# Queries and keys turned block by block, and maxima over partitions without GpSimd

## The chip, the cores and the metric

One core of a Trainium2 chip runs the kernel. The metric is the device time of one launch in microseconds (us), from the first to the last instruction of the core and what lies around them. Lower is better.

## The reference

Two layers of a hybrid backbone for 2048 latent tokens and 256 context tokens (2304 together, context first) with 1024 channels. Cut to what matters here:

```python
def hybrid_layer(h, hc, ...):                       # called twice
    lat = split_cols((rms_norm(h, norm_g) * (1 + scale) + shift) @ w_in)     # 1024 -> 3584
    cx  = split_cols((rms_norm(hc, norm_g) * (1 + scale_c) + shift_c) @ w_in)
    att_l, att_c = gqa_branch(lat[4], lat[5], lat[6], cx[4], cx[5], cx[6], q_g, k_g, cos, sin, need_ctx)
    hg_l, hg_c = hgrn_branch(...)                   # gated recurrence in both directions
    y_conv, y_four, g_att, g_hg = mix_stream(lat, conv_w)   # short convolution, 2-D Fourier, gates
    y = concatenate([y_conv, att_l * g_att, hg_l * g_hg, y_four]) @ w_out
    return h + gate * y, ...

def gqa_branch(...):                                # 4 query heads, 2 key heads, 64 wide
    ql = apply_rope(rms_norm(to_heads(q_l, 4), q_g), cos, sin)
    kl = apply_rope(rms_norm(to_heads(k_l, 2), k_g), cos, sin)
    # latent queries attend to latent and context keys; context queries to context keys
    # (the context output is needed in the first layer only)
```

Everything is float32 in the reference. The kernel does its large products in float16 pairs (a high part and what is left over), with power-of-two scales that are taken from the largest absolute value of a tensor.

## The kernel before

One instruction stream per engine is written out by nested generators (`weave` interleaves several by their shares of the work), and a list scheduler may then move instructions of independent tiles past each other. DMAs all go through SyncE's queue (SPq in the profile).

A layer goes through these stages: a recurrence stage over nine blocks of 256 tokens (`hg_proj`, `hg_levels`, with the norms of the next tokens), the reverse recurrence (`hg_reverse`), the Fourier branch, a stage that makes the attention's queries, keys and values and the gates (`att_block`, `gate_block`), and then attention in jobs of 512 queries, woven with the convolution blocks and the output projection. The first layer's attention stage runs from about 700 us to 1370 us, the second's from about 2040 us to the end.

**Weights.** Each of the 14 blocks of `w_in` per layer goes through `wprep`: two loads of 512 KB into `wst` (line 368), `wsplit` takes the largest absolute value of each partition on VectorE (line 142, two instructions, joined in line 378), `allmax` takes the maximum over the 128 partitions with a GpSimd all-reduce (line 136), `pow2` makes the scale (lines 124 to 130), and ScalarE and VectorE write the high and low part (lines 389, 390). `allmax` is called 32 times in all: for 28 weight blocks, for the two layers' modulation (`mod_finish`) and for the two layers' values (`att_load`).

**GpSimd's other work.** `rpow` (line 151) takes the power -0.5 on GpSimd, for the norms (`nrr`), for the recurrence's output (`hrr`, used in line 739) and for queries and keys (`arr`, used in line 828).

**Queries and keys.** After `att_rope` a block's keys are stored token by token into the DRAM tensor `d_k` with the columns (high, high, low) and padding, the queries into `d_qt` likewise (lines 852, 859, 860: two, two and two stores per block). The padding itself, zeros and two columns of 64, is written by 36 small stores at the start (`load_masks`, lines 231 and 232). When attention opens, `att_load` turns the keys with four transposing DMAs from DRAM (line 869) and `att_fetch` turns the queries of a job with one (line 888: 512 tokens by 1024 columns). `att_max` (line 901) finds each query's largest score; its results go by DMA into two more rows of the second query operand (lines 920, 923), so that the second score product (line 977) subtracts them.

Of the kernel before, what the change touches and what calls it, by code (L numbers as in the profile page):

```python
# [4 lines left out]

# [7 lines left out]
F16 = mybir.dt.float16  # L13
F32 = mybir.dt.float32
# [4 lines left out]
ALU = mybir.AluOpType  # L19
# [6 lines left out]
NCX = 256  # L26
# [47 lines left out]
class Net:  # L74
# [57 lines left out]
        return s[:, 0:1], s[:, 1:2]  # L132

    def allmax(self, a):
        r = self.t(self.small, [128, 1], F32, "allmax")
        self.nc.gpsimd.partition_all_reduce(r, a, channels=128, reduce_op=bass_isa.ReduceOp.max)
        return r

    def absmax(self, src, pool=None):
# [15 lines left out]
    def setup(self):  # L155
# [4 lines left out]
        nc.vector.tensor_copy(out=self.id16, in_=self.id32)  # L160
        self.mhalf = cst.tile([128, 24], F32, name="mhalf")
        nc.vector.memset(self.mhalf, -0.5)
        self.pshift = cst.tile([128, 1], F32, name="pshift")
        nc.vector.memset(self.pshift, PSHIFT)
        self.cact = cst.tile([128, 32, 8], F32, name="cact")
# [48 lines left out]
        self.d_op = dt("d_op", [NT, 256])  # L214
        self.d_qb = dt("d_qb", [NTT, 128, 256])

        self.d_qt = dt("d_qt", [NT, 2, 4, 128], F16)
        self.d_k = dt("d_k", [NT, 2, 256], F16)
        self.d_v = dt("d_v", [NTT, 128, 128])
        self.d_gate = dt("d_gate", [2, 2, D])  # L220

    def load_masks(self, pool):
        nc = self.nc
        nc.sync.dma_start(out=self.masks, in_=self.ap["masks"])

        pad = self.t(pool, [128, 2, 4, 64], F16, "pad", 1)
        nc.gpsimd.memset(pad, 0.0)
        nc.gpsimd.memset(pad[:, 1, 0:2, 0:2], MROW)
        for t in range(NTT):
            r = slice(t * 128, t * 128 + 128)  # L230
            nc.sync.dma_start(out=self.d_qt[r, 1, :, 64:128], in_=pad[:, 0])
            nc.sync.dma_start(out=self.d_k[r, :, 192:256], in_=pad[:, 1, 0:2])


    def mod_load(self, l, c0, n, pool, bufs=2):
# [136 lines left out]
    def wsplit(self, l, b, half, pool=None, pace=False):  # L372

        nc = self.nc
        slow = self.paced if pace else ExitStack
        with slow():
            am = self.absmax(half[0])
            nc.vector.tensor_tensor(out=am, in0=am, in1=self.absmax(half[1]), op=ALU.max)
            ds = self.t(self.small, [128, 4], F32, "ds", bufs=16)
            sw, isw = self.pow2(self.allmax(am), self.small, tag="sw")  # L380
            nc.vector.tensor_copy(out=ds[:, 3:4], in_=isw)
        yield
        for i, st in enumerate(half):
            with slow():
                if i == 0:
                    wh = self.t(pool or self.wpool, [128, KC, 256], F16, "wh")
                    wl = self.t(pool or self.wpool, [128, KC, 256], F16, "wl")
                k = slice(4 * i, 4 * i + 4)
                a = nc.scalar.activation(out=wh[:, k], in_=st, func=AF.Copy, scale=sw)  # L389
                v = nc.vector.scalar_tensor_tensor(out=wl[:, k], in0=st, scalar=sw, in1=wh[:, k], op0=ALU.mult, op1=ALU.subtract)  # L390
            if i == 0:
                yield
        self.W[b] = (wh, wl, ds)
        self.wlast = (a, v)
        if self.mod[l] is not None:
            self.wscale(l, self.W[b])
        yield
# [367 lines left out]
    def att_open(self, l, pool):  # L765
        nc = self.nc
        self.atp = pool
        self.apend = []
# [12 lines left out]
        nc.vector.scalar_tensor_tensor(out=self.ascale, in0=inv[0], scalar=0.125, in1=inv[1], op0=ALU.mult, op1=ALU.mult)  # L781
        self.rope = self.t(pool, [128, 2, 16, 32], F32, "rope", 1)
        nc.sync.dma_start(out=self.rope, in_=self.ap["rope"])

    def att_block(self, l, sb):
# [15 lines left out]
        if needq:  # L801
            h0 = 0
            pq = self.bank("mm")
            for j in range(2):
                yield from self.mm_tok(pq[:, j * 256 : j * 256 + 256], wq, sb * 2 + j)
            nc.scalar.activation(
                out=x[:, :, 0:4], in_=pq.rearrange("p (j h d) -> p j h d", j=2, h=4), func=AF.Copy, scale=wq[2][:, 0:1]
            )
        nh = 6 - h0
        xv = x[:, :, h0:6]  # L810
        sq = self.t(pool, [128, 2, 6, 64], F32, "asq", 2)
# [10 lines left out]
    def att_rope(self, sb, x, r, h0):  # L822
# [20 lines left out]
                nc.vector.tensor_tensor(out=tmp, in0=xp[:, :, :, :, 1], in1=tab(1 - e), op=ALU.mult)  # L843
                nc.vector.tensor_tensor(out=yp[:, :, :, :, e], in0=yp[:, :, :, :, e], in1=tmp, op=o)

        kt = self.t(pool, [128, 2, 2, 192], F16, "akt", 2)
        yk = y[:, :, 4:6]
        nc.vector.tensor_copy(out=kt[:, :, :, 0:64], in_=yk)
        nc.vector.tensor_copy(out=kt[:, :, :, 64:128], in_=kt[:, :, :, 0:64])
        nc.vector.tensor_sub(out=kt[:, :, :, 128:192], in0=yk, in1=kt[:, :, :, 0:64])  # L850
        for j in range(2):
            nc.sync.dma_start(out=self.d_k[sb * 256 + j * 128 : sb * 256 + j * 128 + 128, :, 0:192], in_=kt[:, j])
        if h0 == 0:
            q = self.t(pool, [128, 2, 4, 128], F16, "aqt", 2)
            nc.vector.tensor_copy(out=q[:, :, :, 64:128], in_=y[:, :, 0:4])
            nc.vector.tensor_sub(out=q[:, :, :, 0:64], in0=y[:, :, 0:4], in1=q[:, :, :, 64:128])
            for j in range(2):
                r = slice(sb * 256 + j * 128, sb * 256 + j * 128 + 128)
                nc.sync.dma_start(out=self.d_qt[r, 0], in_=q[:, j])
                nc.sync.dma_start(out=self.d_qt[r, 1, :, 0:64], in_=q[:, j, :, 64:128])  # L860

    def att_load(self, keep, pool):

        nc = self.nc

        self.K = self.t(keep, [128, 4, NT], F16, "K12", 1)
        self.V = self.t(keep, [128, NTT, 2, 129], F16, "V", 1)
        for a, b in ((0, NCX), (NCX, 768), (768, 1536), (1536, NT)):
            nc.sync.dma_start_transpose(out=self.K[:, :, a:b], in_=self.d_k[a:b].rearrange("t h x -> t (h x)"))
        nc.vector.memset(self.V[:, :, :, 64:65], 1.0)  # L870
        am = self.t(self.small, [128, 1], F32, "amax")
        nc.vector.tensor_reduce(out=am, in_=self.vmax, axis=AX.X, op=ALU.max)
# [9 lines left out]
    def att_fetch(self, job, pool):  # L882

        nc = self.nc
        n = job["nq"] * 128
        r = slice(job["tq"] * 128, job["tq"] * 128 + n)
        job["Q"] = self.t(pool, [128, 8, 512], F16, "Q12", 2)
        nc.sync.dma_start_transpose(out=job["Q"][:, :, :n], in_=self.d_qt[r].rearrange("t k h x -> t (k h x)"))
        yield

    def att_max(self, job, pool):

        nc = self.nc
        nq, nk, Q = job["nq"], job["nk"], job["Q"]
        chunks = [(c, min(512, nk * 128 - c)) for c in range(0, nk * 128, 512)]
        mx = self.t(pool, [128, 4, nq, len(chunks)], F32, "amx", 2)
        for j in range(nq):
            for h in range(4):
                for i, (c, w) in enumerate(chunks):
                    ps = self.bank("tr")  # L900
                    nc.tensor.matmul(ps[:, :w], lhsT=Q[:, h, j * 128 : j * 128 + 128], rhs=self.K[:, h // 2 * 2, c : c + w], start=True, stop=True)  # L901
# [15 lines left out]
        for e in range(2):  # L917
            src = mt[4 * nq * e : 4 * nq * e + 4 * nq]
            if nq == 4:
                nc.sync.dma_start(out=Q[64 + e : 65 + e, 4:8], in_=src)  # L920
            else:
                for h in range(4):
                    nc.sync.dma_start(out=Q[64 + e : 65 + e, 4 + h, : nq * 128], in_=src[nq * h : nq * h + nq])
        yield

    def att_core(self, job, pool):
# [1 line left out]
        nc = self.nc  # L928
        tq, nq, nk = job["tq"], job["nq"], job["nk"]
        n = nq * 128  # L930
        Q = job["Q"]
        dst = {}

        def values(h, s, ph, pl):
# [33 lines left out]
        for h in range(4):  # L968
            kv = h // 2
            for s in range(nk):  # L970
# [5 lines left out]
                nc.tensor.matmul(ps[:, :n], lhsT=self.K[:, 2 * kv, c], rhs=Q[:, h, :n], start=True, stop=False)  # L976
                nc.tensor.matmul(ps[:, :n], lhsT=self.K[:66, 2 * kv + 1, c], rhs=Q[:66, 4 + h, :n], start=False, stop=True)  # L977
# [335 lines left out]
    def layer(self, l, L, R, tail):  # L1313
# [33 lines left out]
        with ExitStack() as st:  # L1347
# [3 lines left out]
            if l == 0:  # L1351
# [11 lines left out]
                self.load_masks(nm)  # L1363
            else:
                self.wlast = ()
            self.hg_open(l, hgk)
# [18 lines left out]
        def late():  # L1385


            def gen():
                self.att_rope(*self.apend.pop(0))
                yield  # L1390

            return 1, gen()
# [180 lines left out]
```

## Time and profile before

| | |
|---|---|
| median of three runs | 2719.91 us (2716.54 to 2721.13) |
| the profiled execution, own time | 2729.11 us |
| its span, first to last instruction | 2727.3 us |
| mean granted TensorE clock | 0.979 of full speed |
| TensorE matmul busy | 2591.0 us (95%) |
| VectorE busy | 2060.0 us (76%) |
| ScalarE busy | 1495.7 us (55%) |
| GpSimd busy | 118.2 us (4%) |

Busy time of TensorE counts pipelined matmuls whose ends are modelled, so 95% says that it hardly ever has nothing in flight, not that it is at its peak. What to look for in this profile is the 136 us in which TensorE does nothing, and what it waits for then.

### The profile page before, as it was taken

The page shows a single profiled execution, that of the slowest core. Times are in us where ns is not written, and L with a number is a line of the kernel's source. Part 1 is how long each engine was busy: PE and PEld are TensorE (multiplying, and loading weights), DVE is VectorE, ACT ScalarE, POOL GpSimd, SP SyncE. Part 2 cuts the span into 40 slices and gives each one's busy share as a digit, 9 for nine tenths or more (in the row PEclk, how much of TensorE's full clock was granted, in tenths as well). Part 3 has the DMA queues.
Part 4 walks back from the last instruction along what each step waited for, and adds up shares of the span by engine and source line. Part 5 has one row for each costly group of instructions (what it writes and reads, how often), then busy time and mean ns, then how long its engine had stood idle before and what let it go on. Part 6 is the DMA issues. An engine that isn't in the chain of part 4 may idle for free.

```text
span 2727.3 us, 67225 instructions
## 1 busy us (share of the span) xinstructions
PE 2591.0 (95%) x28142; PEld 2045.1 (75%) x28142; DVE 2060.0 (76%) x4534; ACT 1495.7 (55%) x2823; POOL 118.2 (4%) x140
## 2 busy tenths in 40 slices
PE   5899999999899999999989999989998999999998
PEld 3788877788677876666678788878886787666677
DVE  5888864656686678898776888866678766999874
ACT  3777642322316557698736666523221655879872
POOL 0000001011000000000000000010110000000000
PEclk8899999999899999999999999999999999999999
DMA  8111168322610032312161111343324102221223
GB/s 238 62 49 52 33 199 269 119 81 77 145 35 25 24 102 81 99 57 75 65 210 63 45 49 36 105 136 120 85 76 88 44 24 59 95 77 57 75 83 109
DMA packets 260232, 240.32 MB, mean 88 GB/s; under 512 B 107093, under 2 KB 232025, under 8 KB 259929
## 3 DMA queue, kind: packets, MB, share of 16 engines
q1 hardware_dynamic: 259928, 236.04, 28.0%
q8 instruction: 220, 3.60, 0.6%
q14 instruction: 84, 0.68, 0.1%
HBM read 149.98 MB, written 72.30 MB: 82 GB/s over the span
## 4 chain that ended last, share of the span: by engine, by line
PE 67%; DVE 14%; ACT 6%; DMA 5%; issue 4%; SPq 2%; POOL 2%; POOLq 0%; DVEq 0%; ACTq 0%
PE psmm L1245 12%; PE psmm L414 6%; PE psmm L415 6%; PE psmm L416 6%; PE pstr L901 4%; PE psmm L430 4%; PE psmm L428 4%; PE psmm L429 4%; PE pspv L943 4%; PE pssc L976 4%; PE pssc L977 4%; PE pspv L944 2%; PE pspv L689 2%; ACT aP L979 1%; DMA wmod<-w_mod 1%
## 5 line engine op out<-in xcount | busy, mean ns | idle before, releaser
L414 PE MATMUL psmm<-xh,wh 128*128 128x256 f16 x2208 | 609.8, 276 | 13.8 <-DVE xh L344 7.0
L415 PE MATMUL psmm<-xl,wh 128*128 128x256 f16 x2208 | 608.6, 276 | 1.5 <-DVE xl L345 1.5
L416 PE MATMUL psmm<-xh,wl 128*128 128x256 f16 x2208 | 608.4, 276 | 0.0
L979 ACT ACTIVATE aP<-pssc,pshift,ascale 128x512 f32<-128x512 f32 (+1 forms) x584 | 446.4, 779 | 244.8 <-PE pssc L977 228.4
L986 DVE TENSOR_TENSOR apl<-aP,aph 128x512 f16<-128x512 f32 (+1 forms) x584 | 392.0, 682 | 104.6 <-ACT aph L985 97.1
L428 PE MATMUL psmm<-wh,xh 128*128 128x256 f16 x1664 | 456.0, 274 | 2.5 <-ACT wh L389 1.9
L902 DVE TENSOR_REDUCE amx<-pstr 128x1 f32<-128x512 f32 (+1 forms) x648 | 391.9, 627 | 87.0 <-PE pstr L901 84.5
L429 PE MATMUL psmm<-wl,xh 128*128 128x256 f16 x1664 | 455.4, 274 | 1.1 <-DVE wl L390 1.1
L430 PE MATMUL psmm<-wh,xl 128*128 128x256 f16 x1664 | 455.5, 274 | 0.0
L985 ACT CAST aph<-aP 128x512 f16<-128x512 f32 (+1 forms) x508 | 307.2, 620 | 10.3
L943 PE MATMUL pspv<-V,aph 128*128 128x129 f16 x2320 | 296.3, 222 | 0.4 <-ACT ao L954 0.4
L943 PEld LDWEIGHTS <-aph 128*128 128x128 f16 x2320 | 211.4, 97 | 83.0 <-issue 47.9
L944 PE MATMUL pspv<-V,apl 128*128 128x65 f16 x2320 | 269.6, 193 | 2.8 <-DVE apl L986 2.2
L415 PEld LDWEIGHTS <-wh 128*128 128x128 f16 x2208 | 218.3, 99 | 67.7 <-issue 14.5
L414 PEld LDWEIGHTS <-wh 128*128 128x128 f16 x2208 | 218.7, 99 | 56.2 <-issue 6.7
L901 PE MATMUL pstr<-K,Q 128*128 128x512 f16 (+1 forms) x648 | 229.3, 362 | 28.4 <-issue 19.7
L416 PEld LDWEIGHTS <-wl 128*128 128x128 f16 x2208 | 218.2, 99 | 34.8 <-issue 2.4
L944 PEld LDWEIGHTS <-apl 128*128 128x128 f16 x2320 | 208.4, 98 | 44.2 <-DVE apl L986 14.7
L1245 PE MATMUL psmm<-xh,oyh 128*128 128x512 f32 x544 | 239.2, 440 | 0.1
L1245 PE MATMUL psmm<-xl,oyh 128*128 128x512 f32 x544 | 238.5, 438 | 0.0
L976 PE MATMUL pssc<-Q,K 128*128 128x512 f16 (+1 forms) x584 | 221.8, 380 | 3.3 <-ACT aP L979 2.3
L977 PE MATMUL pssc<-Q,K 66*128 66x512 f16 (+1 forms) x584 | 222.6, 384 | 0.5 <-DMA Q<-amt 0.4
(279 smaller groups left out, 4304.4 us busy)
## 6 DMA issues: line engine op xcount, KB each, us to landing
wst<-w_in SPq DMA_DIRECT2D x56, 512.0 KB
wmod<-w_mod SPq DMA_DIRECT2D x18, 1024.0 KB
d_G<-nh SPq DMA_DIRECT2D x51, 256.0 KB
oo<-d_O SPq DMA_DIRECT2D x34, 384.0 KB
og<-d_G SPq DMA_DIRECT2D x34, 384.0 KB
d_h<-oh SPq DMA_DIRECT2D x18, 512.0 KB
nh<-d_h SPq DMA_DIRECT2D x18, 512.0 KB
nh<-x SPq DMA_DIRECT2D x16, 512.0 KB
```

Of the source, the lines that this page charges most:

```text
L414: nc.tensor.matmul(out, lhsT=wh[:, k, cs], rhs=a, start=(k == 0), stop=False)
L415: nc.tensor.matmul(out, lhsT=wh[:, k, cs], rhs=b, start=False, stop=False)
L416: nc.tensor.matmul(out, lhsT=wl[:, k, cs], rhs=a, start=False, stop=(k == KC - 1))
L428: nc.tensor.matmul(out, lhsT=a, rhs=wh[:, k, :], start=(k == 0), stop=False)
L429: nc.tensor.matmul(out, lhsT=a, rhs=wl[:, k, :], start=False, stop=False)
L430: nc.tensor.matmul(out, lhsT=b, rhs=wh[:, k, :], start=False, stop=(k == KC - 1))
L902: nc.vector.tensor_reduce(out=mx[:, h, j, i : i + 1], in_=ps[:, :w], axis=AX.X, op=ALU.max)
L943: nc.tensor.matmul(pv(j), lhsT=ph[:, t], rhs=self.V[:, s, kv, :], start=st, stop=False, skip_group_check=True)
L944: nc.tensor.matmul(pv(j)[:, 0:65], lhsT=pl[:, t], rhs=self.V[:, s, kv, 0:65], start=False, stop=sp and j % 2 == 1, skip_group_check=True)
L979: nc.scalar.activation(out=P[:, :n], in_=ps[:, :n], func=AF.Exp, scale=self.ascale, bias=self.pshift)
L986: nc.vector.tensor_sub(out=pl[:, :n], in0=P[:, :n], in1=ph[:, :n])
L1245: nc.tensor.matmul(ps, lhsT=y, rhs=w, start=(i == 0), stop=(i == len(mms) - 1))
```

## The change

The maximum over partitions becomes three steps: `rowmax` turns the 128 values into one row of PSUM with a TensorE transpose and VectorE reduces that row to one value; `spread` multiplies a row of ones with that value on TensorE, which puts it on all partitions, and VectorE copies it out of PSUM. In `wsplit` the two are in different steps of the generator.

Queries and keys are turned as soon as a block has them: `att_rope` writes high and low part beside each other and turns them with four transposing DMAs from SBUF to SBUF per block (two of 128 by 256 for the keys, two of 128 by 512 for the queries). `att_store` writes the turned block to DRAM one block later, with one store for the keys and one for the queries. When attention opens, six plain loads bring in the keys and three plain loads the queries of a job. The constant rows are written by a VectorE memset, and the 36 padding stores are gone.

```diff
     def allmax(self, a):
+        return self.spread(self.rowmax(a))
+    def rowmax(self, a):
+        nc = self.nc
+        pt = self.bank("tr")
+        nc.tensor.transpose(pt[:1, :128], a, self.id32)
+        m = self.t(self.small, [1, 1], F32, "rowmax")
+        nc.vector.tensor_reduce(out=m, in_=pt[:1, :128], axis=AX.X, op=ALU.max)
+        return m
+    def spread(self, m):
+        nc = self.nc
+        pt = self.bank("tr")
+        nc.tensor.matmul(pt[:, 0:1], lhsT=self.ones, rhs=m, start=True, stop=True)
         r = self.t(self.small, [128, 1], F32, "allmax")
-        self.nc.gpsimd.partition_all_reduce(r, a, channels=128, reduce_op=bass_isa.ReduceOp.max)
+        nc.vector.tensor_copy(out=r, in_=pt[:, 0:1])
         return r
...
-        self.d_qt = dt("d_qt", [NT, 2, 4, 128], F16)
-        self.d_k = dt("d_k", [NT, 2, 256], F16)
+        self.d_qt = dt("d_qt", [128, 4, NT], F16)
+        self.d_kt = dt("d_kt", [128, 2, NT], F16)
...
-        for t in range(NTT):
-            r = slice(t * 128, t * 128 + 128)
-            nc.sync.dma_start(out=self.d_qt[r, 1, :, 64:128], in_=pad[:, 0])
-            nc.sync.dma_start(out=self.d_k[r, :, 192:256], in_=pad[:, 1, 0:2])
...
-            sw, isw = self.pow2(self.allmax(am), self.small, tag="sw")
+            m = self.rowmax(am)
+        yield
+        with slow():
+            sw, isw = self.pow2(self.spread(m), self.small, tag="sw")
             nc.vector.tensor_copy(out=ds[:, 3:4], in_=isw)
-        yield
...
+        if self.tpend:
+            self.att_store()
...
-        kt = self.t(pool, [128, 2, 2, 192], F16, "akt", 2)
...
-            nc.sync.dma_start(out=self.d_k[sb * 256 + j * 128 : sb * 256 + j * 128 + 128, :, 0:192], in_=kt[:, j])
...
-                nc.sync.dma_start(out=self.d_qt[r, 0], in_=q[:, j])
-                nc.sync.dma_start(out=self.d_qt[r, 1, :, 0:64], in_=q[:, j, :, 64:128])
+        t = [(y[:, :, 4:6], 2, "k", self.d_kt)]
         if h0 == 0:
+            t.append((y[:, :, 0:4], 4, "q", self.d_qt))
+        for src, n, tag, dst in t:
+            a = self.t(pool, [128, 2, n, 128], F16, f"a{tag}s", 2)
+            nc.vector.tensor_copy(out=a[:, :, :, 0:64], in_=src)
+            nc.vector.tensor_sub(out=a[:, :, :, 64:128], in0=src, in1=a[:, :, :, 0:64])
+            b = self.t(pool, [128, n, 256], F16, f"a{tag}t", 2)
             for j in range(2):
+                nc.sync.dma_start_transpose(out=b[:, :, j * 128 : j * 128 + 128], in_=a[:, j].rearrange("p h x -> p (h x)"))
+            self.tpend.append((b, dst, sb))
+    def att_store(self):
+        while self.tpend:
+            b, dst, sb = self.tpend.pop(0)
+            self.nc.sync.dma_start(out=dst[:, :, sb * 256 : sb * 256 + 256], in_=b)
...
-        self.K = self.t(keep, [128, 4, NT], F16, "K12", 1)
+        self.K1 = self.t(keep, [128, 2, NT], F16, "K1", 1)
+        self.K2 = self.t(keep, [66, 2, NT], F16, "K2", 1)
-        for a, b in ((0, NCX), (NCX, 768), (768, 1536), (1536, NT)):
-            nc.sync.dma_start_transpose(out=self.K[:, :, a:b], in_=self.d_k[a:b].rearrange("t h x -> t (h x)"))
+        nc.vector.memset(self.K2[64:66], MROW)
+        for a, b in ((0, NCX), (NCX, 1024), (1024, NT)):
+            nc.sync.dma_start(out=self.K1[:, :, a:b], in_=self.d_kt[:, :, a:b])
+            nc.sync.dma_start(out=self.K2[:64, :, a:b], in_=self.d_kt[:64, :, a:b])
...
-        nc.sync.dma_start_transpose(out=job["Q"][:, :, :n], in_=self.d_qt[r].rearrange("t k h x -> t (k h x)"))
+        for r in range(2):
+            nc.sync.dma_start(out=Q1[64 * r : 64 * r + 64, :, :n], in_=self.d_qt[0:64, :, c])
+        nc.sync.dma_start(out=Q2[0:64, :, :n], in_=self.d_qt[64:128, :, c])
...
                 self.att_rope(*self.apend.pop(0))
                 yield
+                self.att_store()
+                yield
```

The first `att_store` of the diff stands in `att_block` ahead of its `rpow`; the last hunk is `late`, the step that turns the last block. The score products keep their shapes; they read `K1`, `Q1` and `K2`, `Q2` instead of slices of one tile.

## Rows read from the trace of the kernel before

**Rows 1.** The page: span, and busy time of each engine with its share of the span and its instructions.

```profile
span 2727.3 us, 67225 instructions
PE 2591.0 (95%) x28142; PEld 2045.1 (75%) x28142; DVE 2060.0 (76%) x4534; ACT 1495.7 (55%) x2823; POOL 118.2 (4%) x140
```

**Rows 2.** Stretches of the span: us, busy time of TensorE matmul, TensorE weight load, VectorE, ScalarE and GpSimd with their instructions, granted TensorE clock, share of the DMA engines, GB/s.

```profile
590.00:700.00 110.00, 110.00 (x1008) 98.44 (x1007) 70.12 (x159) 31.54 (x48) 18.73 (x11) 1.00 0.24 66
725.00:730.00 5.00, 5.00 (x32) 3.73 (x30) 3.54 (x9) 0.00 (x0) 0.00 (x0) 0.65 1.12 216
495.00:500.00 5.00, 3.87 (x19) 3.03 (x20) 4.00 (x5) 0.65 (x2) 0.03 (x1) 0.52 0.35 103
1400.00:1405.00 5.00, 3.85 (x15) 3.32 (x16) 4.54 (x10) 2.50 (x7) 0.38 (x1) 0.56 0.49 166
1820.00:1825.00 5.00, 3.46 (x43) 2.38 (x43) 2.61 (x7) 2.08 (x5) 1.64 (x1) 0.58 0.47 146
```

**Rows 3.** TensorE's matmuls in order of time, those that follow a long idle time: start, us, operation; in brackets the idle time before and what ended it.

```profile
496.13 1.22 PE L1082 MATMUL pstr<-fch,fu 128*128 128x128 f32 x4 [5.07 <-DVE modrow L260]
...
724.67 0.59 PE L901 MATMUL pstr<-K,Q 128*128 128x256 f16 x2 [11.83 <-issue]
...
1005.11 1.03 PE L901 MATMUL pstr<-K,Q 128*128 128x512 f16 x2 [2.11 <-DMA Q<-d_qt]
...
1401.15 1.11 PE L333 MATMUL pstr<-id,nh 128*128 128x128 f32 x4 [8.41 <-DVE oyl L1235]
...
1797.22 1.03 PE L720 MATMUL pspv<-hst,hKc 64*64 64x64 f32 x28 [2.94 <-DVE hQc L732]
...
1821.54 0.37 PE L414 MATMUL psmm<-xh,wh 128*128 128x256 f16 x1 [5.59 <-ACT fu L1067]
...
2055.57 0.58 PE L901 MATMUL pstr<-K,Q 128*128 128x512 f16 x1 [7.87 <-issue]
...
2308.01 0.60 PE L901 MATMUL pstr<-K,Q 128*128 128x512 f16 x2 [2.08 <-DMA Q<-d_qt]
```

**Rows 4.** GpSimd in order of time, the same columns.

```profile
458.38 1.64 POOL L151 TENSOR_TENSOR hrr<-hrv,mhalf 128x8 f32<-128x8 f32 x1 [11.11 <-DVE hrv L149]
...
485.55 0.38 POOL L136 PARTITION_ALL_REDUCE allmax<-amax  x1 [5.85 <-issue]
493.35 1.68 POOL L151 TENSOR_TENSOR hrr<-hrv,mhalf 128x8 f32<-128x8 f32 x1 [7.42 <-issue]
...
1807.67 0.38 POOL L136 PARTITION_ALL_REDUCE allmax<-amax  x1 [6.21 <-DVE hst L448]
1815.78 1.68 POOL L151 TENSOR_TENSOR hrr<-hrv,mhalf 128x8 f32<-128x8 f32 x1 [7.73 <-issue]
```

**Rows 5.** VectorE in order of time, the instructions that use a result of GpSimd's power.

```profile
460.05 0.69 DVE L739 TENSOR_TENSOR hQc<-hQc,hrr 128x512 f32<-128x512 f32 x1 [1.81 <-POOL hrr L151]
...
495.07 0.69 DVE L739 TENSOR_TENSOR hQc<-hQc,hrr 128x512 f32<-128x512 f32 x1 [5.26 <-POOL hrr L151]
...
698.08 0.96 DVE L828 TENSOR_TENSOR ax<-ax,arr 128x768 f32<-128x768 f32 x1 [6.18 <-POOL arr L151]
...
1397.19 1.58 DVE L316 TENSOR_SCALAR nh<-nh,nrr 128x1024 f32<-128x1024 f32 x2 [4.19 <-POOL nrr L151]
...
1794.15 0.69 DVE L739 TENSOR_TENSOR hQc<-hQc,hrr 128x512 f32<-128x512 f32 x1 [3.81 <-POOL hrr L151]
...
1817.50 0.69 DVE L739 TENSOR_TENSOR hQc<-hQc,hrr 128x512 f32<-128x512 f32 x1 [7.51 <-POOL hrr L151]
```

**Rows 6.** VectorE in order of time, around one maximum over partitions of GpSimd (first two) and around one small TensorE transpose of eight columns, whose input and output these are (last two).

```profile
370.15 0.15 DVE L378 TENSOR_TENSOR amax<-amax,amax 128x1 f32<-128x1 f32 x1
370.78 0.15 DVE L124 TENSOR_SCALAR p2e<-allmax 128x1 uint32<-128x1 uint32 x1 [0.49 <-POOL allmax L136]
...
731.75 0.16 DVE L909 TENSOR_TENSOR ams<-am,ams 128x8 f16<-128x8 f32 x1
...
732.23 0.21 DVE L916 COPY amt<-pstr 16x128 f16<-16x128 f16 x1
```

**Rows 7.** Line 914, the small transposes of attention's maxima: duration in ns (least, median, most), and, below, the time in us and the number of times that their engine sat idle until VectorE had their input.

```profile
L914 PE MATMUL pstr<-id,ams x9: 223/230/230, 732.0 to 2540.6; 128*32 128x128 f16 x8, 128*16 128x128 f16 x1
...
  DVE ams L909: 2.5, 7
```

**Rows 8.** The costliest groups, the instructions that take the largest absolute value of half a weight block: busy us, mean ns of one, idle time before.

```profile
L142 DVE TENSOR_REDUCE amax<-wst 128x1 f32<-128x1024 f32 x56 | 66.6, 1211 | 10.8 <-DMA wst<-w_in 10.7
```

**Rows 9.** SyncE's queue in order of time: start, us of issuing, operation, number of DMAs. The first row and the row at 64.58 us have the 36 padding stores of lines 231 and 232 between them.

```profile
33.12 0.50 SPq L224 DMA_DIRECT2D masks<-masks  x1
...
64.58 29.98 SPq L309 DMA_DIRECT2D nh<-x  x6
...
706.22 2.37 SPq L852 DMA_DIRECT2D d_k<-akt  x2
...
710.93 4.21 SPq L869 DMA_TRANSPOSE K<-d_k  x2
...
719.79 6.77 SPq L888 DMA_TRANSPOSE Q<-d_qt  x2
...
998.95 3.93 SPq L888 DMA_TRANSPOSE Q<-d_qt  x1
...
2045.81 3.93 SPq L888 DMA_TRANSPOSE Q<-d_qt  x1
```

More of the change, by code (lines that the diff above doesn't have):

```diff
@@ L6 @@
 import concourse.bass as bass
-import concourse.bass_isa as bass_isa
 import concourse.tile as tile
@@ L162, in setup @@
         nc.vector.memset(self.mhalf, -0.5)
+        self.ones = cst.tile([1, 128], F32, name="ones")
+        nc.vector.memset(self.ones, 1.0)
         self.pshift = cst.tile([128, 1], F32, name="pshift")
@@ L215, in setup, with load_masks @@
         self.d_qb = dt("d_qb", [NTT, 128, 256])
-        self.d_qt = dt("d_qt", [NT, 2, 4, 128], F16)
-        self.d_k = dt("d_k", [NT, 2, 256], F16)
+        self.d_qt = dt("d_qt", [128, 4, NT], F16)
+        self.d_kt = dt("d_kt", [128, 2, NT], F16)
         self.d_v = dt("d_v", [NTT, 128, 128])
         self.d_gate = dt("d_gate", [2, 2, D])
[L222 to L228, printed above, removed]
-        for t in range(NTT):
-            r = slice(t * 128, t * 128 + 128)
-            nc.sync.dma_start(out=self.d_qt[r, 1, :, 64:128], in_=pad[:, 0])
-            nc.sync.dma_start(out=self.d_k[r, :, 192:256], in_=pad[:, 1, 0:2])
+    def load_masks(self):
+        self.nc.sync.dma_start(out=self.masks, in_=self.ap["masks"])
     def mod_load(self, l, c0, n, pool, bufs=2):
@@ L767, in att_open @@
         self.atp = pool
-        self.apend = []
+        self.apend, self.tpend = [], []
         self.vmax = self.t(self.cst, [128, NTT // 2], F32, "vmax", 1)
@@ L844, in att_rope @@
                 nc.vector.tensor_tensor(out=yp[:, :, :, :, e], in0=yp[:, :, :, :, e], in1=tmp, op=o)
-        kt = self.t(pool, [128, 2, 2, 192], F16, "akt", 2)
[L847 to L851, printed above, removed]
-            nc.sync.dma_start(out=self.d_k[sb * 256 + j * 128 : sb * 256 + j * 128 + 128, :, 0:192], in_=kt[:, j])
@@ L853, in att_rope @@
-        if h0 == 0:
-            q = self.t(pool, [128, 2, 4, 128], F16, "aqt", 2)
-            nc.vector.tensor_copy(out=q[:, :, :, 64:128], in_=y[:, :, 0:4])
-            nc.vector.tensor_sub(out=q[:, :, :, 0:64], in0=y[:, :, 0:4], in1=q[:, :, :, 64:128])
-            for j in range(2):
-                r = slice(sb * 256 + j * 128, sb * 256 + j * 128 + 128)
-                nc.sync.dma_start(out=self.d_qt[r, 0], in_=q[:, j])
-                nc.sync.dma_start(out=self.d_qt[r, 1, :, 0:64], in_=q[:, j, :, 64:128])
+        t = [(y[:, :, 4:6], 2, "k", self.d_kt)]
@@ L885, in att_fetch @@
         n = job["nq"] * 128
-        r = slice(job["tq"] * 128, job["tq"] * 128 + n)
-        job["Q"] = self.t(pool, [128, 8, 512], F16, "Q12", 2)
-        nc.sync.dma_start_transpose(out=job["Q"][:, :, :n], in_=self.d_qt[r].rearrange("t k h x -> t (k h x)"))
+        c = slice(job["tq"] * 128, job["tq"] * 128 + n)
+        Q1 = self.t(pool, [128, 4, 512], F16, "Q1", 2)
+        Q2 = self.t(pool, [66, 4, 512], F16, "Q2", 2)
+        for r in range(2):
+            nc.sync.dma_start(out=Q1[64 * r : 64 * r + 64, :, :n], in_=self.d_qt[0:64, :, c])
+        nc.sync.dma_start(out=Q2[0:64, :, :n], in_=self.d_qt[64:128, :, c])
+        job["Q"] = (Q1, Q2)
         yield
@@ L893, in att_max @@
         nc = self.nc
-        nq, nk, Q = job["nq"], job["nk"], job["Q"]
+        nq, nk, (Q1, Q2) = job["nq"], job["nk"], job["Q"]
         chunks = [(c, min(512, nk * 128 - c)) for c in range(0, nk * 128, 512)]
@@ L900, in att_max @@
                     ps = self.bank("tr")
-                    nc.tensor.matmul(ps[:, :w], lhsT=Q[:, h, j * 128 : j * 128 + 128], rhs=self.K[:, h // 2 * 2, c : c + w], start=True, stop=True)
+                    nc.tensor.matmul(ps[:, :w], lhsT=Q1[:, h, j * 128 : j * 128 + 128], rhs=self.K1[:, h // 2, c : c + w], start=True, stop=True)
                     nc.vector.tensor_reduce(out=mx[:, h, j, i : i + 1], in_=ps[:, :w], axis=AX.X, op=ALU.max)
@@ L919, in att_max @@
             if nq == 4:
-                nc.sync.dma_start(out=Q[64 + e : 65 + e, 4:8], in_=src)
+                nc.sync.dma_start(out=Q2[64 + e : 65 + e], in_=src)
             else:
                 for h in range(4):
-                    nc.sync.dma_start(out=Q[64 + e : 65 + e, 4 + h, : nq * 128], in_=src[nq * h : nq * h + nq])
+                    nc.sync.dma_start(out=Q2[64 + e : 65 + e, h, : nq * 128], in_=src[nq * h : nq * h + nq])
         yield
@@ L930, in att_core @@
         n = nq * 128
-        Q = job["Q"]
+        Q1, Q2 = job["Q"]
         dst = {}
@@ L975, in att_core @@
                 ps = self.bank("sc")
-                nc.tensor.matmul(ps[:, :n], lhsT=self.K[:, 2 * kv, c], rhs=Q[:, h, :n], start=True, stop=False)
-                nc.tensor.matmul(ps[:, :n], lhsT=self.K[:66, 2 * kv + 1, c], rhs=Q[:66, 4 + h, :n], start=False, stop=True)
+                nc.tensor.matmul(ps[:, :n], lhsT=self.K1[:, kv, c], rhs=Q1[:, h, :n], start=True, stop=False)
+                nc.tensor.matmul(ps[:, :n], lhsT=self.K2[:, kv, c], rhs=Q2[:, h, :n], start=False, stop=True)
                 P = self.t(pool, [128, 512], F32, "aP", 3)
@@ L1362, in layer @@
                         run(block, 9 if i == 0 else 8)
-                self.load_masks(nm)
+                self.load_masks()
             else:
@@ L1390, in gen @@
                 yield
-            return 1, gen()
+                self.att_store()
+                yield
+            return 2, gen()
         preps = lambda bs, pool=None: chain(*[(4, self.wprep(l, b, pool, b < 4)) for b in bs])
```

## The prediction, on record before the changed kernel was run

> **What bounds the kernel now.** I read the page first. TensorE is busy for 2591.0 of 2727.3 us [rows 1], so the kernel can only get faster through the 136 us in which TensorE stands still, through the clock, or through less work on TensorE, and the change adds work there. Then I read the stretches: from 590 to 700 us, where queries, keys and weights are made, TensorE is busy all 110 us at full clock, while VectorE has 70 and GpSimd 19 [rows 2]. Whatever is saved on VectorE or GpSimd in such a stretch is worth nothing. So I went through TensorE's matmuls in order of time and kept those after a long pause [rows 3], and for each asked what VectorE or the DMA queue did in it. They are of two kinds.
>
> The first kind is behind GpSimd. Its all-reduce and its power each take 0.4 to 2 us, but when one follows the other, 5.85 us pass before it (485.55) and then 7.42 us before the next (493.35), put down to nothing but "issue"; between two powers the wait is VectorE's (458.38, brought by `hrv`) [rows 4]. [...] VectorE, which works in order, sits in front of the result: 1.81 us in the ordinary case (460.05), 5.26, 3.81 and 7.51 us where a maximum came just before (495.07, 1794.15, 1817.50), 4.19 us at 1397.19 [rows 5]. TensorE's pauses of 5.07, 8.41, 2.94 and 5.59 us stand at just those places [rows 3].
>
> The second kind is behind the transposing loads. When attention opens, TensorE waits 11.83 us (724.67) and, in the second layer, 7.87 us (2055.57); the three later query fetches cost some 2 us each (1005.11, 2308.01) [rows 3]. SyncE's queue shows why: the last block's stores go out from 706.22, the keys' transposes from 710.93, the first queries' only at 719.79, and issuing one takes 2.1 to 3.9 us [rows 9].
>
> [...]
>
> **The sum, part by part,** against the profiled execution's own 2729.1 us (1.8 us more than its span; it was 0.34% above the median of the runs, and I scale the result down by that).
>
> *Without GpSimd's turns.* VectorE's wait falls to the ordinary 1.81 us. At 496 us that frees 5.26 - 1.81 = 3.4 us of TensorE's 5.07; at 1797, 2.0 of 2.94; at 1821, 5.7 of which TensorE can use its 5.59. At 1401 the wait of 4.19 goes, and a late maximum before it too; the bounds are 4.2 and the whole 8.41, and I take 6.0, since VectorE has a queue of other work there. [...] At the start of the kernel the first powers come some us earlier, but loads and ScalarE stand beside it: 1.0. Sum: 3.4 + 2.0 + 5.6 + 6.0 + 3.0 + 1.0 = 21.0 us gained. The wait at 698.08 (6.18 us [rows 5]) is counted with the opening below.
>
> *What replaces it.* TensorE gets a transpose and a product per maximum. The nearest matmul is that of line 914, 0.23 us [rows 7], of which the next matmul hides a part, as matmuls start every 0.11 us [rows 2] though each lasts longer; between nothing and 0.46 for both I take 0.27, for the 24 of 32 that fall where TensorE is full (not the first five, nor three at the second layer's start): 6.5 us. Second, TensorE too works in order: a transpose that stands in its queue before VectorE has finished the two 1.21 us reductions [rows 8] stops every projection matmul behind it, and ScalarE's and VectorE's evacuations wait for those. The nearest row is again line 914, also a transpose of a small VectorE result: 2.5 us of waiting for nine of them, 0.28 each [rows 7]. The bounds are nothing and the whole 2.6 us of reducing; I take the 0.28, as the scheduler that orders both is the same: 28 x 0.28 = 7.8 us. Third, the round trip itself. From the end of the last VectorE step to the first use GpSimd needs 0.48 us (370.30 to 370.78); one bounce off TensorE takes 0.32 (731.91 to 732.23), and two with VectorE's reduction of 0.2 between make 0.9 to 1.0 [rows 6]. That 0.5 us is hidden wherever TensorE has projections to do, that is nearly everywhere; four maxima stand on the path at the start, 2.0 us. Sum: 16.3 us lost.
>
> [...]
>
> *The openings.* The last block's rope starts at 698.08 after 6.18 us of waiting [rows 5], against 1.81 in the ordinary case, so in the first layer it ends some 4 us earlier, at 702 rather than 706. Then come four small transposes (of issuing each between the 0.50 us of a plain load and the 2.1 of a larger transpose [rows 9]; I take 0.6, they have an eighth to a quarter of its size), their landing, some 2 us (6.16 less 3.93 for the fetch at 998.95, below), two to four stores, and nine or twelve plain loads at 0.50, in place of the transposes' 4.21 + 6.77 us and more [rows 9]. The stores wait for the transposes, and behind them in SyncE's queue stand the loads and the gates' stores. All that the first product needs but the last block is in DRAM long before. [...] If they stand behind the stores (702 + 2.4 + 2 + 1) and the keys' 1.8 MB (8.3 us at the 216 GB/s of [rows 2]), the first queries land near 719, and some 5 of 11.83 us go. I take 8 in the first layer; in the second, where the rope ends hardly earlier and all of a 512-query job must be there, 4 of 7.87 (bounds 0 and 9.4). Gain 12 us. A memset of two rows of 4608 values is new on VectorE; between nothing and the 1.2 ns a value of the reductions [rows 8], 5.4 us, in a stretch where VectorE mostly waits: 1 us lost in all.
>
> *The query fetches.* The transpose takes 6.16 us from issue to first use (998.95 to 1005.11) [rows 3, 9]. Three plain loads of 256 KB run side by side; I take 1 us less each, with bounds of 0 and 2.1 (the pause): 3 us gained.
>
> *Nothing:* the 36 padding stores keep SyncE's queue until 64.58 us [rows 9], but ScalarE has weight splits to do until about then; without that cover it would be worth up to 4 us. In the making of queries and keys VectorE saves a copy and SyncE has six stores less per block, four transposes and two stores more; TensorE is full there [rows 2].
>
> Together: -21.0 + 16.3 - 12.0 + 1.0 - 3.0 = -18.7 us, so 2710.4 us, 0.69% less; from the median, 2701 us.
>
> **The rivals.** (a) *Everything clears:* no waiting in TensorE's queue (7.8 more), both openings gone (11.2 more), fetches hidden (3 more) and all 8.41 us at 1401 (2.4 more): -43 us, 2677. For it: the scheduler keeps VectorE-fed transposes fed elsewhere. (b) *TensorE waits for the reductions:* if the queue's order puts the transpose as little as 0.95 us too early on average, 28 x 0.95 eats the whole gain; at 1.5 us the sum is +15.5 us, 2735. For it: `rowmax` follows the reductions in the same step, line 914 has two empty steps ahead. Against it: the 0.28. (c) *The openings stay:* the loads stand behind the last block's transposes and stores, which now land one after the other; then 12 + 3 us are missing, -3.7 us, 2716. (d) *The small transposes are slow:* at 2.1 us of issuing, the smallest step of [rows 9], the last block's four take 8.4 us to issue and, if they run one after the other, as long to land, 16.8 in place of 4.4; both openings are 12.4 us later than in the sum, -18.7 + 24.8 = +6.1 us, 2726.
>
> [...]
>
> **Numbers.** Chances: forecast 0.45, (a) 0.20, (b) 0.12, (c) 0.16, (d) 0.07. Measurements of this kernel can tell about 0.2%, 5.4 us. Faster than 2714.5: nearly all of the forecast, (a) and just under half of (c), 0.71. Within: the rest of (c) for the most part and some of (d), 0.11. Slower: (b), most of (d), 0.18. The range goes from (a) to a little above (d), 2677 to 2728, and leaves out (b) and what lies below (a).
>
> **What would show it.** Right: no "issue" pauses of 6 us ahead of line 151, VectorE's wait at 739 at 1.8 us throughout, TensorE's pauses near 496 and 1821 under 2 us, the first product of line 901 within 4 us of the last projection. Wrong: TensorE idle put down to the reductions of line 142 or 378 in the stretch that is full now, or first products of attention still some 10 us late, behind transposes or stores in SyncE's queue. [...]

## The result: slower by 1.2%, and the profile after

The changed kernel takes 2751.94 us in the median (2751.09 to 2754.18), the kernel before 2720.05 beside it. The ratio is 1.0115, 95% interval 1.0102 to 1.0129. I had forecast 2701 and gave 0.18 to slower.

The page after, its span and busy times as in [rows 1]:

```profile
span 2752.3 us, 67292 instructions
PE 2616.4 (95%) x28238; PEld 2059.1 (75%) x28238; DVE 2078.0 (75%) x4583; ACT 1496.6 (54%) x2823; POOL 105.3 (4%) x106
```

TensorE stands still for the same 136 us as before; its busy time has grown by 25 us with 96 matmuls more. Part of that busy time is a low clock; the mean granted clock is 0.979, as before. The waits of TensorE and VectorE, added up (who waited for whom: us, times, longest):

```profile
PE pstr L140 <- DVE amax L385: 26.3, 8, 6.2
PE pstr L148 <- DVE cm L1034: 9.5, 1, 9.5
PE pstr L148 <- DVE rowmax L142: 8.7, 3, 8.0
...
DVE hQc L748 <- POOL hrr L165: 29.5, 17, 1.8
...
DVE allmax L150 <- PE pstr L148: 15.4, 13, 4.6
```

Line 140 is the transpose of a maximum, line 148 the spreading product, line 385 the join of VectorE's two reductions. Eight transposes wait 3.3 us each on average. VectorE's wait for GpSimd's power at line 748 never exceeds 1.8 us now, where [rows 5] has up to 7.51; at line 839, for queries and keys, the longest is 2.4 us, where it was 6.18.

Three of the eight stand in the stretch from 590 to 700 us, which TensorE filled before [rows 2]. The four of the first layer's stage in TensorE's order of time, and the spreading product of V's maximum at the opening:

```profile
560.49 0.37 PE L140 MATMUL pstr<-id,amax 128*1 128x128 f32 x1 [3.02 <-DVE amax L385]
607.36 0.27 PE L140 MATMUL pstr<-id,amax 128*1 128x128 f32 x1 [3.17 <-DVE amax L385]
658.10 0.27 PE L140 MATMUL pstr<-id,amax 128*1 128x128 f32 x1 [2.98 <-DVE amax L385]
696.70 0.27 PE L140 MATMUL pstr<-id,amax 128*1 128x128 f32 x1 [3.16 <-DVE amax L385]
735.61 0.58 PE L148 MATMUL pstr<-rowmax,ones 1*128 1x1 f32 x2 [9.48 <-DVE cm L1034]
```

VectorE around the wait at 658.10:

```profile
655.04 2.33 DVE L156 TENSOR_REDUCE amax<-wst 128x1 f32<-128x1024 f32 x2
657.29 0.68 DVE L766 SCALAR_TENSOR_TENSOR nh<-nh 128x512 f32<-128x512 f32 x1
657.89 0.15 DVE L385 TENSOR_TENSOR amax<-amax,amax 128x1 f32<-128x1 f32 x1
...
662.24 0.16 DVE L150 COPY allmax<-pstr 128x1 f32<-128x1 f32 x1 [2.20 <-PE pstr L148]
```

TensorE ran dry at 655.1, just as VectorE began to reduce; it had nothing but the transpose at the head of its queue. The spreading product then stood behind projections until 661.6, and VectorE waited 2.20 us in its turn. The stretches, columns as in [rows 2]:

```profile
590.00:700.00 110.00, 100.70 (x873) 87.37 (x872) 65.06 (x136) 26.37 (x40) 14.78 (x6) 0.96 0.29 75
...
659.20:663.00 3.80, 3.80 (x21) 2.66 (x19) 1.49 (x7) 0.84 (x2) 0.00 (x0) 0.55 0.54 139
663.00:667.00 4.00, 4.00 (x39) 3.59 (x38) 3.17 (x10) 1.15 (x1) 0.00 (x0) 1.00 0.32 98
```

A microsecond after the pause the granted clock falls to 0.55 (the matmuls from 659.56 to 662.54 start some 0.21 us apart, those up to 659.40 and from 662.92 on 0.11): 21 matmuls fall in 3.8 us where 37 would at the pace of the next 4 us, 16 x 0.11 = 1.8 us lost. The 8 us behind each of the four pauses are granted 0.79, so the price is much the same for all. A wait of 3.1 us thus costs about 4.9. Three of them make 14.6 us (the low clock behind the third lies in part after 700), and the stretch has 135 matmuls fewer than before, which is 14.8.

The first opening, VectorE and then SyncE's queue in order of time:

```profile
717.93 0.69 DVE L863 TENSOR_TENSOR aqs<-ay,aqs 128x512 f16<-128x512 f32 x1
...
729.62 0.06 DVE L1033 MEMSET cu<- 128x4 f32 x1 [6.41 <-DMA d_qt<-aqt]
...
730.73 3.90 DVE L882 MEMSET K<- 2x4608 f16 x1 [1.01 <-DMA K<-d_kt]
734.66 0.69 DVE L766 SCALAR_TENSOR_TENSOR nh<-nh 128x512 f32<-128x512 f32 x1
```

```profile
720.36 2.47 SPq L866 DMA_TRANSPOSE akt<-aks  x2
722.88 2.56 SPq L866 DMA_TRANSPOSE aqt<-aqs  x2
...
726.86 0.51 SPq L873 DMA_DIRECT2D d_qt<-aqt  x1
...
735.38 0.37 SPq L767 DMA_DIRECT2D d_G<-nh  x1
737.80 1.18 SPq L906 DMA_DIRECT2D Q<-d_qt  x2
```

The last queries are ready at 718.6; four transposes take 5.0 us to issue, their store follows at 726.86, and VectorE's memset of the convolution's buffer, which lies in the memory of the transposed block, waits for it. Behind it stand the 3.90 us memset of K2's constant rows and the last gate's product, behind that the gate's store, and then the query loads. From the queries to attention's first product of line 921 (745.2) it is 26.6 us; before, from 706.8 to 724.67 [rows 3], 17.9.

### The profile page after: what moved, and what is told of

Same layout as the page of the kernel before. It is cut to its first block, busy times and chain, and to the rows that moved or that the text cites. A ratio compares the mean times of both kernels' runs of the same rounds, so it can differ in the third digit from the quotient of the medians.

```text
span 2752.3 us, 67292 instructions
## 1 busy us (share of the span) xinstructions
PE 2616.4 (95%) x28238; PEld 2059.1 (75%) x28238; DVE 2078.0 (75%) x4583; ACT 1496.6 (54%) x2823; POOL 105.3 (4%) x106
```

## Experiments

Theory 1: transposes that stand in TensorE's queue before VectorE has reduced cost the time, by the wait and the low clock behind it. Theory 2: at the openings V's maximum, K2's memset and what hangs on them. Theory 3: the block-by-block turning. Theory 4: the added instructions themselves. The kernel before took 2726 to 2728 us beside these runs, not 2720, so the ratios are compared, each with its 95% interval.

**The parts alone.** `turn_only` is the changed kernel with

```
-            m = self.rowmax(am)
-        yield
-        with slow():
-            sw, isw = self.pow2(self.spread(m), self.small, tag="sw")
+            sw, isw = self.pow2(self.allmax(am), self.small, tag="sw")
             nc.vector.tensor_copy(out=ds[:, 3:4], in_=isw)
+        yield
```

and `allmax` by `partition_all_reduce`; `max_only` is the kernel before with the changed kernel's `rowmax`, `spread` and splitting of the weights.

> The changed kernel with every maximum back on GpSimd; only the block-by-block turning is left of the change. Theory 1 (the time went where TensorE's queue holds a transpose that waits for VectorE's reductions, and at the two openings to V's maximum in the same queue): the 32 us lost in the two projection stages are not there, the 21 us gained without GpSimd's turns are not there either, the three query fetches keep their 4 us: 2706 to 2716 us, against 2720 before. Rival, theory 3 (the turning costs the time: four transposes and two stores for each block in SyncE's queue, late stores, the memset): the loss of 14 us at the openings and a part of that in the projections stay: 2728 us or more.

> The kernel before with the maxima taken by TensorE, VectorE and the spreading product; queries and keys are turned as before. Theory 1: GpSimd's turns give 21 us back, the waiting transposes with the low clock behind them cost 32 us in the two projection stages, and V's maximum holds TensorE's queue at the openings as in the changed kernel or less: 2728 to 2745 us. Theory 3 (the turning is to blame): only the gain is seen, 2698 to 2710 us.

Turning alone: 2729.17 us, 1.0015 (1.0006 to 1.0024). Maxima alone: 2747.12, 1.0077 (1.0065 to 1.0089), with line 140 waiting 25.6 us in eight times. So the maxima carry the loss, as theory 1 has it. But the turning is not the gain that theory 1 left for it: it costs 4 us, between the two theories. Where, the traces do not show: from the last rope's start to the first product it is 32.0 and 28.2 us in the two layers, before 26.6 and 25.8, but the pauses just ahead of that product are 9.53 and 9.62 us, before 11.83 and 7.87, and the profiled execution (2725.65 us) is no slower than that of the kernel before (2729.11).

**A transpose that needs not wait.** `const_turn`; the weights' scale is that of a maximum of 1, the rest is computed:

```
-            m = self.rowmax(am)
+            m = self.rowmax(self.id32[:, 0:1])
```

> The changed kernel, but the transpose of a weight block's maximum reads a column of the identity matrix, which has long been there, and not the block's own maximum (the scale of the weights is then that of a maximum of 1). VectorE's reductions, and every other instruction, stay. Theory 1: TensorE never waits for VectorE there: the eight waits (26.3 us) and the low clock behind them (some 2 us each) go: 2709 to 2728 us. Rival, theory 4 (the 96 added TensorE instructions, the second wait for the spreading product, or something else in the stage cost the time): within 6 us of 2752.

2718.52 us, 0.9970 (0.9959 to 0.9981): 1.45% under the changed kernel, some 39 us. That is near what the eight waits and the low clock behind each add up to (26.3 + 8 x 1.8 = 41, an estimate that takes the 1.8 for all). Theory 4 falls as the cause of the loss: every instruction is still there. This run also frees the splitting of the weights from the reductions; the next one keeps that tie.

**The same transpose, later.** `late_turn`:

```
             ds = self.t(self.small, [128, 4], F32, "ds", bufs=16)
+        yield
+        with slow():
             m = self.rowmax(am)
```

with the counts of the weaving raised from 4 to 5 steps a block.

> The changed kernel with the transpose of a weight block's maximum put one step of the weaving later than the reductions, so that some 6 us of projections stand between them in TensorE's queue. Theory 1: the waits of line 140 go, as with the constant column: 2709 to 2730 us. Rival (the wait only moves, to the spreading product or to VectorE's own queue, which is late with something else): above 2740 us.

2719.40 us, 0.9973 (0.9964 to 0.9983). The waits and the full stage in the trace of `late_turn`:

```profile
PE pstr L140 <- DVE amax L385: 3.1, 2, 1.9
...
DVE allmax L150 <- PE pstr L148: 20.3, 22, 3.8
```

```profile
590.00:700.00 110.00, 110.00 (x1005) 98.06 (x1003) 76.05 (x166) 30.55 (x46) 17.23 (x7) 1.00 0.33 84
```

The stretch is as full as before, 1005 matmuls at full clock, ten of them the added ones. One block there reads so on VectorE, reductions first, and its transpose on TensorE at 640.53, 6.5 us after the join, without a wait:

```profile
631.46 2.33 DVE L156 TENSOR_REDUCE amax<-wst 128x1 f32<-128x1024 f32 x2
633.83 0.16 DVE L385 TENSOR_TENSOR amax<-amax,amax 128x1 f32<-128x1 f32 x1
...
644.42 0.27 DVE L142 TENSOR_REDUCE rowmax<-pstr 1x1 f32<-1x128 f32 x1
```

VectorE now waits more often for the spreading product (20.3 us, not 15.4); there it costs nothing that shows.

**More to reduce.** `double_reduce` repeats the first half's reduction twice in each block:

```
             am = self.absmax(half[0])
+            nc.vector.tensor_reduce(out=am, in_=half[0], axis=AX.XY, op=ALU.max, apply_absolute_value=True)
+            nc.vector.tensor_reduce(out=am, in_=half[0], axis=AX.XY, op=ALU.max, apply_absolute_value=True)
```

> The changed kernel with two more of VectorE's reductions of the first half block (1.2 us each) ahead of each weight block's maximum, nothing else. Theory 1 (TensorE stands at the transpose as long as VectorE reduces): the eight waits grow by up to 2.4 us each: 12 to 24 us more than the changed kernel, 2764 to 2780 us. Rival (the price of a turn is fixed, or VectorE's work is hidden as it was in the kernel before): within 6 us of 2751.

2772.62 us, 1.0164 (1.0151 to 1.0177): 0.49% more than the changed kernel, 13 us, at the low end of theory 1. Its size was not as I said: line 140 waits 30.8 us in 12 times, not 26.3 in 8, so 4.5 of the 13 us are waiting there; the rest I have not separated. TensorE's pauses in the first layer's stage:

```profile
572.22 0.37 PE L140 MATMUL pstr<-id,amax 128*1 128x128 f32 x1 [5.12 <-DVE amax L387]
622.01 0.37 PE L140 MATMUL pstr<-id,amax 128*1 128x128 f32 x1 [3.45 <-DVE amax L387]
673.37 0.37 PE L140 MATMUL pstr<-id,amax 128*1 128x128 f32 x1 [3.26 <-DVE amax L387]
713.09 0.27 PE L140 MATMUL pstr<-id,amax 128*1 128x128 f32 x1 [3.45 <-DVE amax L387]
```

Only the first has grown by the added 2 us. At 622.01 ScalarE's evacuation of the next projections ran at 616.86, ahead of the transpose, where it had come after it (608.21): the transpose now stands a group later in the queue. The wait is thus not simply the time of reducing, but how much too early the order puts the transpose.

**The openings.** On the late version, each run adds one edit to the one ahead:

```
-        s, self.visc = self.pow2(self.allmax(am), keep, tag="avs")
+        g = self.t(self.small, [128, 1], F32, "vall")
+        nc.gpsimd.partition_all_reduce(g, am, channels=128, reduce_op=bass_isa.ReduceOp.max)
+        s, self.visc = self.pow2(g, keep, tag="avs")
...
-        nc.vector.memset(self.K2[64:66], MROW)
+        nc.gpsimd.memset(self.K2[64:66], MROW)
...
-            nc.vector.memset(u[:, :, 0:2], 0.0)
+            nc.gpsimd.memset(u[:, :, 0:2], 0.0)
```

(`late_v_gp`, `late_v_k2_gp`, and `late_open`, which moves the other border columns too); and `v_k2_gp` has the first two in the changed kernel itself.

> The changed kernel with the late transpose, and V's maximum at the two openings of attention back on GpSimd. Theory 2 (V's spreading product stands in TensorE's queue ahead of the convolution's products, and waits for VectorE's reduction behind the memset of K2: 9.45 us at 714.4, 3.3 and 2.9 us in the second layer, in the run with the late transpose): 6 to 13 us less than that run, 2706 to 2714. Rival: TensorE then waits for something else at the same place (VectorE's memset of the convolution's buffers, which waits 6.4 us for the queries' last store, or the query loads at 717.5): within 4 us of 2719.

> As the kernel with the late transpose and V's maximum on GpSimd, and the memset of K2's two constant rows (3.90 us on VectorE) on GpSimd as well. Theory 2: VectorE starts the convolution's evacuations some 4 us earlier in each layer: 2 to 8 us less than without. Rival: VectorE has time there, no difference (within 2 us); or GpSimd takes longer for the memset and holds V's maximum back behind it: slower.

> The changed kernel itself (early transposes in the projection stages), with V's maximum and the memset of K2's constant rows on GpSimd. Theory 2: the openings' 9.48 and 7.98 us of TensorE waiting for the spreading product go, at least in half: 2734 to 2746 us against 2752. Theory 1 alone (the openings are late for other reasons): within 4 us of 2752.

> The changed kernel with the late transpose, and at the opening of attention V's maximum, K2's memset and the memsets of the convolution's border columns on GpSimd. Theory 2b (the openings are a chain: the last block's transposes and stores, VectorE's memset of the convolution's buffer that waits 6.4 to 7.1 us for the queries' last store, the last gate's product behind it in VectorE's queue, that gate's store, and only then the query loads, which take the gate's memory; 715.28 in the run with V's maximum and K2's memset on GpSimd): with the memset out of VectorE's queue the query loads go out 3 to 6 us earlier in the first layer: TensorE's wait of 11.8 us there falls to 6 to 9, the time to 2710 to 2718. Rival (the loads wait for something else, the last block's stores or SyncE's own queue): the query loads stay near 715, no difference from 2722.

0.9987 (0.9976 to 0.9998), 0.9987 (0.9978 to 0.9995), 1.0084 (1.0070 to 1.0097) and 0.9985 (0.9976 to 0.9993). Theory 2 falls on the late version: V's maximum on GpSimd gains nothing over `late_turn`, and TensorE's pause at the same place is now put down to the query loads (9.54 us at 729.09). In the changed kernel it gives 0.3%, 8 us and by the ratio within theory 2's range (its own 2749.59 us lies outside, but the kernel before took 2726.68 beside it), yet not by theory 2's way: the pauses of 9.48 and 7.98 us are gone, and in their places stand 8.77 (query loads) and 9.11 (key loads). Where those 8 us come from I have not found. Theory 2b falls as well: in `late_open` the last gate's product is ready at 705.76, yet in SyncE's queue its store stands behind the key loads:

```profile
703.95 2.57 SPq L869 DMA_TRANSPOSE aqt<-aqs  x2
...
708.57 0.60 SPq L887 DMA_DIRECT2D K<-d_kt  x1
...
710.78 0.58 SPq L770 DMA_DIRECT2D d_G<-nh  x1
...
715.14 1.18 SPq L911 DMA_DIRECT2D Q<-d_qt  x2
```

`late_act` issues that store and the first query loads from ScalarE:

```
-        nc.sync.dma_start(
+        q = nc.scalar if b == 11 and sb == NTT // 2 - 1 else nc.sync
+        q.dma_start(
             out=self.d_G[sb * 256 : sb * 256 + 256, col : col + 256]
...
+        q = nc.scalar if job["tq"] <= 2 else nc.sync
```

> As the run with the borders' memsets on GpSimd (0.15% under the kernel before; there the last gate's product was ready at 705.8, but its store was issued at 710.78 and the query loads at 715.14), with that last store and the first query loads issued from ScalarE's queue, past SyncE's. Theory 2c (SyncE's queue, with the last block's transposes, stores and the key loads in order, holds the openings): the query loads go out at 708 to 711 in the first layer, TensorE's wait of 12.2 us falls to 4 to 8, and the kernel is 0.25 to 0.5% faster than before. Rival (the query loads wait for the last block's own stores to land, or TensorE for its own queue): the first product stays within 2 us of 720.6 and the time does not move.

1.0015 (1.0005 to 1.0025), slower than without it: theory 2c falls. ScalarE's queue, then SyncE's store of the last block's queries and GpSimd's memset that waits for it:

```profile
712.85 0.40 ACTq L771 DMA_DIRECT2D d_G<-nh  x1
717.69 1.28 ACTq L913 DMA_DIRECT2D Q<-d_qt  x2
```

```profile
714.30 0.51 SPq L877 DMA_DIRECT2D d_qt<-aqt  x1
...
717.83 0.10 POOL L1040 MEMSET cu<- 128x4 f32 x1 [20.95 <-DMA d_qt<-aqt]
```

The gate's store had landed by 715.1, as the semaphores in the trace show. The query loads wait now for the last block's own queries, whose store landed at 717.5: the first half of the rival that I had named. TensorE then waits for the keys (14.32 us at 727.38). From the last rope's start to the first product it is 30.5 us, in `late_open` 29.7. Each wait taken away uncovers the next. Which part of the openings' loss is the transposes' own and which the order of memory behind them stays open.

**The maxima alone, late.** `late_max_only` is the kernel before with the late transpose; `late_max_open` has V's maximum and the borders' memsets on GpSimd too.

> The kernel before (queries and keys turned by its transposing loads), with the maxima taken by TensorE, VectorE and the spreading product, the transpose one step of the weaving after the reductions. The one run so far with turning alone was 0.15% slower than before (4 us), the one with late maxima and turning 0.27% faster (7 us). If the two parts add, late maxima alone give back GpSimd's turns and little else: 11 us less than before, 2709 to 2715 on a median before of 2724. Rival: with V's maximum in TensorE's queue at the openings, the turning is worth something there, or the late maxima cost it; then 2716 to 2722.

> The kernel before (queries and keys turned by its transposing loads) with the late maxima of the weights on TensorE, V's maximum and the memsets of the convolution's border columns on GpSimd. If the turning gives less than the openings lose by it, this one is the fastest: 2706 to 2716 us. If the block-by-block turning is worth its stores, it is slower than the run with the late transpose, the turning and the same memsets on GpSimd.

2719.33 us, 0.9974 (0.9965 to 0.9984), and 0.9991 (0.9982 to 0.9999). The first is as fast as `late_turn`, so with late maxima the turning neither gains nor loses; the parts do not simply add. The second is not the fastest, as it would have been had the turning lost at the openings, nor is it slower than `late_open` (0.9985) beyond the noise. `late_turn` and `late_max_only`, some 0.27% under the kernel before, are the fastest versions that I have.

## Why the prediction was wrong

**The step that failed is TensorE's waiting for the reductions:** 28 x 0.28 = 7.8 us. Measured by the runs with and without it, that waiting is worth 1.45% (`const_turn`) or 1.42% (`late_turn`) in the changed kernel, about 39 us, and 1.03% (28 us) without the turning. I took the wait of line 914 [rows 7] as the nearest row, "as the scheduler that orders both is the same". But line 914 has two empty steps ahead of it and `rowmax` none. The mean wait over the 28 blocks was 26.3 / 28 = 0.94 us, which I had named as the point where rival (b) takes over (0.95); the low clock behind each pause and what follows from it bring it to 1.4 us a block, near the 1.5 for which I had 2735. I had seen the mechanism, priced it, and given it 0.12. The low clock after a pause I had read in [rows 2] and counted as a gain, and not on this side. The 1.0 us of it a pause that stands behind the sum's 3.0 no run shows; for the 1.5 us in the bound of 9.4 and in rival (a), the kernel before shows 15 matmuls from 725.05 to 728.04 that start 0.21 us apart, where those from 728.60 on start 0.11 apart, 15 x 0.10 = 1.5 us as an estimate, and the changed kernel 1.8 us behind the wait at 658.10.

**The openings failed too, by less.** I had -12 us, +1 for the memset and -3 for the fetches; turning alone measures +0.15%, 4 us: 18 us off. Issuing a transpose took 1.24 us for 256 columns and 1.28 for 512 (720.36, 722.88), and not 0.6; I had scaled it by its size. The memset took 3.90 us and not 1, with the last gate behind it. And the last step of the chain, that the memory for the convolution and the queries is handed over only when the last block's and the last gate's stores have landed, I had not followed. This is rival (c)'s mechanism with a loss on top. Rival (d) had the right direction; its 2.1 us was too much. (In rival (a) both openings gone are 11.83 + 7.87 and twice 1.5, 22.7 us, 10.7 more than the 12, not 11.2; nothing hangs on it.)

The last block's four transposes, 12 squares of 128 by 128, took 6.5 us at most: first issue at 720.36, store behind them issued at 726.86.

**GpSimd's turns were right in kind.** No power waits behind an all-reduce any more, though what GpSimd did in the 5.85 and 7.42 us no run shows; the pause at 496 [rows 3] is 1.29 us at 492.81, those at 1401, 1797 and 1821 are under 1.8. With the instructions and round trips I had -12.5 us for this; `late_max_only`, which has little else, measures -0.26%, 7 us. Where the other 5 went no run separates, but the term for the added instructions was too small. Two projection products with a spreading product between them, in a full stretch of `late_max_only`:

```profile
609.90 0.27 PE L450 MATMUL psmm<-wh,xl 128*128 128x256 f16 x1
610.10 0.38 PE L148 MATMUL pstr<-rowmax,ones 1*128 1x1 f32 x2
610.41 0.28 PE L448 MATMUL psmm<-wh,xh 128*128 128x256 f16 x1
```

They start 0.51 us apart and not 0.11, so the product costs 0.40, and the transpose takes one more place of 0.11. That is 0.51 us a maximum where I had 0.27, an estimate of 12.2 us for the 24 that I counted and not 6.5. Two more things are new in that trace: VectorE's 19.5 us of waiting for the spreading product, and a TensorE pause of 2.50 us at 1835.03 (5.56 us at 1854.05 in the changed kernel), where ScalarE's copy of line 1106 waits 5.35 us (8.73) for the store of the recurrence's last output to land.

**The fetches were right.** The pauses of 2.11 and 2.08 us [rows 3] are 0.96 (1019.88) and 0.91; in all, TensorE's wait for query loads fell from 5.9 us in three times to 1.9 in two, 4.0 us where I had 3. The three loads of the first were all issued between 1014.66 and 1016.53, and its first product ran at 1019.88.

The sum with the measured terms: 2701 + (39 - 8) + 18 + 5 = 2755, against 2752 measured. With the 28 us that the waiting costs without the turning it is 2744; as the parts do not simply add, it is partly luck that the first comes so near.

## What to carry to other kernels

Work that GpSimd did was waited for here by its user (up to 7.51 us [rows 5]), and GpSimd's next power came after pauses of 7.42 and 7.73 us [rows 4]; the same work on TensorE, which sets the time, was waited for by everything queued behind it (26.3 us in eight times at line 140, with the low clock behind each). So before moving a small step onto a full in-order engine, look at where its input is ready and put the step a few us behind that: one step of the weaving turned 1.2% slower into 0.3% faster. A pause of 3 us on TensorE should be priced with the low clock behind it, here another 1.8.

## What the runs showed of the hardware

A DMA transpose took about as long to issue for 256 columns (2.47 us for two) as for 512 (2.56).

A memset of 4608 fp16 values on two partitions took 3.90 us on VectorE, 3.93 on GpSimd. While GpSimd ran it in `late_v_k2_gp`, a VectorE instruction lasted 4.01 us, until the memset's end; in the changed kernel, where VectorE runs the memset itself, the same instruction took 0.17 and 0.21 us (737.04, 2075.53). VectorE and GpSimd in the second layer:

```profile
2036.16 4.01 DVE L130 TENSOR_SCALAR avs<-p2f 128x2 uint32<-128x2 uint32 x1
...
2036.21 3.93 POOL L885 MEMSET K<- 2x4608 f16 x1 [18.68 <-issue]
```

By the records VectorE's instruction began 0.05 us before the memset and ended 0.03 us after it; what held it the rows do not show.
